# Hybrid attention encoder layer: where row scaling, the eviction of output tiles and the last weight group's sum stand in the order of group B

## The chip, the cores and the metric

The kernel runs on one core of a Trainium2 chip. A core has five engines with a queue each, which meet only through semaphores: TensorE (PE: matrix products into PSUM; its weight loads are listed apart as PEld), VectorE (DVE), ScalarE (ACT), GpSimd (POOL) and SyncE (SP, which here only starts transfers). Sixteen DMA engines move data. The metric is the device time of one launch in microseconds; the median of the runs shown is 554.95 us. "Before" is the kernel without the change, "after" the one with it.

## What is computed

One mixer layer over 1024 tokens of width 1024, token t at row t // 64 and column t % 64 of a grid:

```python
h = _rmsnorm(x, norm_gain[l])
proj = h @ w_in[l]
q_a, k_a, v_a, g_a, q_b, k_b, v_b, g_b = jnp.split(proj, split_at, axis=-1)
...
o_a = _gqa_blocked(q_a, k_a, v_a) * jax.nn.silu(g_a)
o_b = _neighbourhood_attn(q_b, k_b, v_b, na_rpb[l])
o_b = o_b * jax.nn.silu(g_b)
mixed = jnp.concatenate([o_a, o_b], axis=-1)
x = x + mixed @ w_out[l]
...
return _rmsnorm(x, final_norm_gain)
```

Group A is ordinary attention with 8 query heads over all tokens (after a norm and a rotation of q and k). Group B has 8 heads, and each query sees a window of 8 grid rows by 16 columns, with a learned bias. Both are gated, joined, multiplied by `w_out`, added to x and normed.

## The kernel before

**Tiling.** The tokens are cut into 8 blocks u of 128 (8 grid columns each), so that a block of group B needs the keys of at most three blocks. All matrix products run in float16, each operand split into a high and a low part, so that one product takes three matmuls (hi*hi, hi*lo, lo*hi). The weights come in 17 groups of 256 columns: 0 to 12 from `w_in` (0 k/v of A, 1-2 q of A, 3-4 q of B, 5-6 k of B, 7-8 v of B, 9-10 gate of A, 11-12 gate of B) and 13 to 16 from `w_out`.

**A weight group's way.** `load_w(g)` fetches 1 MB and plans `squares` (L366): four quarters, each an ACT `Square` with its row sum (L372). After the fourth, a job puts g on the list `pend`, `delay` slots later (L374). The next `b_scores` (L825), directly behind its own matmuls, takes g from `pend` and runs `prep_b` (L382): four matmuls with one column (L388) add the squares over the partitions, DVE (L390) and POOL (L391) turn that into a scale. Then `split(g)` (L408) plans four `hi` on ACT (L414), each of which plans a `lo` on DVE (L419). When the last `lo` is done, the group is ready, and one slot later group g+2 is fetched. A matmul that needs the group waits for its pieces.

**Group B.** 32 units (u, p), u in the order 0, 7, 1, 2, 3, 4, 5, 6 and p a pair of heads, run in 36 slots. Slot i does, in the order in which instructions are issued:

- what is planned "pre"; then ACT jobs of up to 1.2 us ("early")
- `b_lo` of unit i-1: DVE L863 makes the low part of the probabilities, SP starts their transposing transfer (L878)
- `b_qk` of unit i: TensorE scores (L833, L836), perhaps `prep_b`, DVE bias and minimum (L854, twice), ACT exponentials (L856, twice) and the high part (L858)
- more ACT jobs, then DVE jobs, then what is planned "post"
- a fill of 24 or 30 projection matmuls (L504): first the eight gate tiles of B, then the output rows
- `b_pv` of unit i-3, from slot 18 on i-4: probabilities times values (L896 to L898)

On every engine this program order is kept through slot 35. The trace shows slot i by its L833. TensorE may run ahead of the others: it stops only where it needs something that they have not done. The scores have four PSUM banks (two are used in each slot), the projections two (`pjb`), the values two (`pvb`).

**The planner.** `Flow.job(engine, cost, fn, delay, late)` makes a job due `delay` slots later. `work` (L91) gives ACT 2.85 and DVE 2.45 units a slot (L130: 1.7 + 0.654 * 4.2 less 1.6 or 2.0). What is left from the slot before is carried, but at most half a budget (1.42 for ACT). Jobs are taken by `late` (smallest first), then by due slot, then by number. A job with `late=0` always runs once it is due; another only if half its cost is below what is left. In the early part `work` stops when 1.2 are spent:

```python
self.left[eng] = 1e9 if b is None else min(self.left.get(eng, 0.0), 0.5 * b) + b
stop = -1e9 if early is None else self.left[eng] - early
```

A square L372 of groups 13 to 16 costs 1.0 (`late=1.2`), a `hi` 0.6 (`late=0.5`), a `put` 0.8, the square L933 0.82, each L946 0.72.

**The places that the change touches.**

- `g_gen` (L700), for B: ACT tanh of the gate (L706), then the job `mul` on DVE (L712), which writes the gated values into `mixB` and marks the half row (pair of blocks, 256 columns) ready. L706 and L712 read the projection tile, so L712 sets it free.
- `evac` in `b_pv_head` (L900): for the four heads of a block, DVE takes the reciprocal of the row sums (L905), scales (L906, L908) and POOL multiplies the result into `mixB` (L910). It sets the `pvb` bank free. If the gate isn't ready, the job is planned again for the next slot, at its cost of 0.85, and there it stands before the gate's `mul`, as its number is smaller.
- `os_start` (L920): as soon as both halves of a block are there, the block's joined row is squared (ACT L933, DVE L938, L940), scaled (POOL L941), split (ACT L946, DVE L950) and transposed for the output product (SP L959).
- `out_gen` (L999): output columns of one or two blocks, 48 matmuls into a projection tile. Then, for the first six blocks from slot 18 on, `put` (L1009): ACT takes the tile out (L1013, twice) and POOL adds it to x (L1019). Each puts the next tile's matmuls off until L1013 is done.

## Time and profile before

| | |
|---|---|
| Median of three runs (lowest, highest) | 554.95 us (553.38, 557.83) |
| The profiled execution: its time, its span | 554.79 us, 553.0 us |
| Mean granted clock of TensorE | 0.989 |
| Group A's end and group B's 36 slots | about 363 to 508 us |
| Output product of the last blocks, final norm | 508 to 553 us |
| TensorE busy, 400 to 450 us | 48.51 of 50 us |
| TensorE busy, 450 to 500 us | 45.42 of 50 us |
| TensorE busy, 500 to 553 us | 45.04 of 53 us |
| VectorE busy, 400 to 450 and 450 to 500 us | 45.44 and 42.10 us |
| ScalarE busy, 400 to 450 and 450 to 500 us | 41.60 and 40.21 us |

The span runs from the first to the last instruction; the time of the execution is 1.8 us longer. In the timeline a row is start, duration, engine, line, operation, out<-in, size, count, and in brackets the idle time before it with what ended it. In the view of waits a row is who waited for whom, the total in us, how often, and the longest. In the chain a row is start, duration, engine, tile and line.

### The profile page before, as it was taken

The page shows a single profiled execution, that of the slowest core. Times are in us where ns is not written, and L with a number is a line of the kernel's source. Part 1 is how long each engine was busy: PE and PEld are TensorE (multiplying, and loading weights), DVE is VectorE, ACT ScalarE, POOL GpSimd, SP SyncE. Part 2 cuts the span into 40 slices and gives each one's busy share as a digit, 9 for nine tenths or more (in the row PEclk, how much of TensorE's full clock was granted, in tenths as well). Part 3 has the DMA queues.
Part 4 walks back from the last instruction along what each step waited for, and adds up shares of the span by engine and source line. Part 5 has one row for each costly group of instructions (what it writes and reads, how often), then busy time and mean ns, then how long its engine had stood idle before and what let it go on. Part 6 is the DMA issues. An engine that isn't in the chain of part 4 may idle for free.

```text
span 553.0 us, 12864 instructions
## 1 busy us (share of the span) xinstructions
PE 507.8 (92%) x5071; PEld 397.2 (72%) x5071; DVE 445.3 (81%) x887; ACT 381.4 (69%) x671; POOL 178.9 (32%) x201
## 2 busy tenths in 40 slices
PE   2657889998999999999999999999999998799994
PEld 0446768876887555558888888988777786589883
DVE  4599678889987888879879898867898997887732
ACT  4545465967887868787787696648688788784411
POOL 1385787581110000101000022634433123344510
PEclk9989999999999999999999999999999999999998
DMA  8997837879999999999997999744897799979722
GB/s 243 210 203 216 146 59 181 135 144 176 208 196 217 191 231 186 216 176 178 194 217 143 202 186 200 120 125 71 146 191 138 136 250 202 219 115 204 173 74 76
DMA packets 244509, 95.40 MB, mean 173 GB/s; under 512 B 235489, under 2 KB 236001, under 8 KB 242530
## 3 DMA queue, kind: packets, MB, share of 16 engines
q1 hardware_dynamic: 242434, 81.23, 80.1%
q0 software_dynamic: 1728, 12.58, 7.3%
q8 instruction: 39, 0.64, 0.5%
q10 hardware_dynamic: 288, 0.79, 0.5%
q14 instruction: 20, 0.16, 0.1%
HBM read 29.56 MB, written 4.19 MB: 61 GB/s over the span
## 4 chain that ended last, share of the span: by engine, by line
PE 50%; DVE 10%; ACT 9%; issue 5%; DMA 3%; POOL 0%; DVEq 0%; POOLq 0%; ACTq 0%
PE pj L504 17%; PE kb L504 7%; PE pjb L504 7%; PE pv L775 5%; PE s L741 4%; PE s L743 4%; ACT rq L856 3%; DVE ar L854 3%; ACT ar L858 2%; PE pv L776 2%; PE sb L504 2%; DMA pt<-ar 2%; DVE ar L863 1%; DMA ar<-ar 1%; DVE whl L419 1%
## 5 line engine op out<-in xcount | busy, mean ns | idle before, releaser
L504 PEld LDWEIGHTS <-hT 128*128 128x128 f16 x2112 | 204.2, 99 | 59.5 <-DMA hT<-ar 16.3
L504 PE MATMUL pj<-whl,hT 128*128 128x256 f16 x1680 | 201.7, 278 | 21.8 <-DMA hT<-ar 9.4
L752 ACT ACTIVATE ar<-s,nm,sm 128x1024 f32<-128x1024 f32 x64 | 76.9, 1201 | 47.7 <-DVE nm L748 45.7
L748 DVE CUSTOM_DVE_ANT_0 ar<-s,sm 128x1024 bf16<-128x1024 f32 x64 | 82.0, 1281 | 30.3 <-PE s L743 28.5
L504 PEld LDWEIGHTS <-ar 128*128 128x128 f16 x768 | 73.8, 98 | 16.0 <-issue 7.8
L758 DVE TENSOR_TENSOR ar<-ar 128x1024 f16<-128x1024 f32 x64 | 79.4, 1241 | 1.2 <-ACT ar L753 1.2
L753 ACT ACTIVATE ar<-ar 128x1024 f16<-128x1024 f32 x64 | 67.6, 1057 | 2.3 <-DVE ar L758 0.4
L504 PE MATMUL pjb<-whl,ar 128*128 128x256 f16 x480 | 56.4, 273 | 2.8 <-ACT whl L414 1.5
L856 ACT ACTIVATE rq<-ar,nm 128x384 f32<-128x384 f32 (+1 forms) x64 | 34.0, 579 | 25.7 <-DVE nm L854 25.1
L504 PE MATMUL pjb<-whl,hT 128*128 128x256 f16 x432 | 50.4, 273 | 0.1
L784 POOL TENSOR_TENSOR ar<-ar,sum 128x256 f32<-128x256 f32 x16 | 11.3, 709 | 110.7 <-DVE ar L783 95.3
L504 PE MATMUL kb<-hT,whl 128*128 128x512 f16 x192 | 44.5, 379 | 0.0
L419 DVE SCALAR_TENSOR_TENSOR whl<-raw,sm,whl 128x512 f16<-128x512 f32 x52 | 41.0, 821 | 2.7 <-ACT whl L414 2.7
L775 PE MATMUL pv<-va,ar 128*128 128x128 f16 x384 | 39.1, 220 | 0.0
L863 DVE SCALAR_TENSOR_TENSOR ar<-rq,ar 128x768 f16<-128x768 f32 (+1 forms) x32 | 29.3, 915 | 11.0 <-ACT ar L858 10.6
L741 PE MATMUL s<-kTa,rq 128*128 128x512 f16 x128 | 38.1, 379 | 0.0
L776 PE MATMUL pv<-va,ar 128*128 128x64 f16 x384 | 37.8, 193 | 0.0
L775 PEld LDWEIGHTS <-ar 128*128 128x128 f16 x384 | 33.9, 98 | 5.3
L776 PEld LDWEIGHTS <-ar 128*128 128x128 f16 x384 | 33.2, 98 | 5.3
L414 ACT ACTIVATE whl<-raw,sm 128x512 f16<-128x512 f32 x52 | 34.0, 709 | 1.4 <-POOL sm L391 1.4
L391 POOL TENSOR_TENSOR sm<-wss,mh 128x1 f32<-128x1 f32 x17 | 10.5, 619 | 72.7 <-DVE wss L390 72.7
L910 POOL TENSOR_TENSOR ar<-ar,qkg 128x256 f32<-128x256 f32 x16 | 17.1, 1072 | 51.6 <-DVE qkg L908 36.4
(174 smaller groups left out, 915.9 us busy)
## 6 DMA issues: line engine op xcount, KB each, us to landing
raw<-in_w_dram POOLq DMA_DIRECT2D x11, 1024.0 KB, 7.6
ar<-in_x_dram SPq DMA_DIRECT2D x7, 512.0 KB, 6.1
raw<-in_wo_dram SPq DMA_DIRECT2D x3, 1024.0 KB, 7.0
khh<-ar SPq DMA_DIRECT2D x16, 128.0 KB, 2.7
x2b<-in_x_dram SPq DMA_DIRECT2D x4, 512.0 KB, 7.4
x<-in_x_dram SPq DMA_DIRECT2D x4, 512.0 KB, 5.6
out_dram<-x2b SPq DMA_DIRECT2D x8, 256.0 KB, 4.1
out_dram<-x SPq DMA_DIRECT2D x7, 256.0 KB, 2.9
```

The lines of the kernel that those rows point to most:

```text
L414: act.activation(wp[g][0][:, q], raw[g][:, q], AF.Copy, scale=col(S_ + g))
L419: dve.scalar_tensor_tensor(wp[g][1][:, q], raw[g][:, q], col(S_ + g), wp[g][0][:, q], op0=OP.mult, op1=OP.subtract)
L504: pe.matmul(*o[0], **o[1])
L741: pe.matmul(s[:, c * 512:(c + 1) * 512], q, kTa[:, 4 * c:4 * c + 4, hh], start=True, stop=False)
L748: dve.tensor_tensor_reduce(out=hl[:, 1].bitcast(BF16), in0=s, in1=col(SHA).to_broadcast([P, 1024]), scale=col(NSA), scalar=3e38, op0=OP.ad ...
L752: act.activation(p32, s, AF.Exp, bias=nm, scale=col(SCA), accum_out=rsum[hh, u][:, h:h + 1])
L753: at(0, "mid", lambda: act.activation(hl[:, 0], p32, AF.Copy))
L758: dve.tensor_tensor(hl[:, 1], p32, hl[:, 0], op=OP.subtract)
L775: pe.matmul(o, pt[:, kt], va[:, kt, hh], start=kt == 0, stop=False)
L776: pe.matmul(o[:, :D], pt[:, 8 + kt], va[:, kt, hh, :D], start=False, stop=kt == 7)
L856: act.activation(p32[:, e], t[:, e], AF.Exp, bias=nm, scale=-1.0)
L863: dve.scalar_tensor_tensor(hl[:, 1], p32, 2.0 ** 14, hl[:, 0], op0=OP.mult, op1=OP.subtract)
```

## The change

Four places are edited, which make three parts.

1. *Rows scaled directly behind their gate.* An `evac` whose gate isn't ready is no longer planned again; it is kept in `held` under its half row. The gate's `mul` plans what is held there at once, for the same slot.
2. *Output rows evicted first.* `put` is no longer a job. It is planned "pre" of the next slot, so it comes before all jobs of ScalarE there, and takes 0.8 from what was left before the cap.
3. *Last weight group's sum.* For group 16 the way from the last square to `pend` takes one slot and not two.

```diff
             if i == 3:
-                job("act", 0, pend.append, g, delay=2 if "b" in late else 1, late=0, key=("sq", g))
+                job("act", 0, pend.append, g, delay=2 if "b" in late and g < 16 else 1, late=0, key=("sq", g))
...
-    mixA, mixB = {}, {}
+    mixA, mixB, held = {}, {}, {}
...
                     dve.scalar_tensor_tensor(m, th, 1.0, pt, op0=OP.add, op1=OP.mult)
                     ready.add((up, cols.start))
+                    for e in held.pop((up, cols.start), ()):
+                        job("dve", 0.85, e, delay=0, late=0)
                     return
...
                 if (u // 2, hh * GC) not in ready:
-                    job("dve", 0.85, evac, late=0)
+                    held.setdefault((u // 2, hh * GC), []).append(evac)
                     return
...
             o = late["ov"][:, k % 2]
+            fl.left["act"] = fl.left.get("act", 0.0) - 0.8
             for i in range(2):
                 act.activation(o[:, i], pt[:, i], AF.Copy, scale=rw[:, i:i + 1])
...
             if "ov" in late and jobs[0][0] in ORDER[:6]:
-                job("act", 0.4 * len(jobs), put, late=0)
+                at(1, "pre", put)
             else:
```

## The prediction, made before the changed kernel had run

> **What bounds the kernel now.** I read the page first, then the waits of TensorE over group B, the chain, and last the timelines of the engines around each wait.

> ```profile
> span 553.0 us, 12864 instructions
> PE 507.8 (92%) x5071; PEld 397.2 (72%) x5071; DVE 445.3 (81%) x887; ACT 381.4 (69%) x671; POOL 178.9 (32%) x201
> ```

> TensorE is busy for 92% of the span, so a gain is a TensorE gap that closes. All three edits act from slot 6 of group B on. There the view of waits, asked for TensorE alone from 360 us to the end, has five lines:

> ```profile
> PE pvb L896 <- DVE qkg L908: 2.0, 4, 0.7
> PE pjb L504 <- ACT pt L1013: 1.8, 1, 1.8
> PE pjb L504 <- ACT whl L414: 1.5, 2, 0.7
> PE pjb L504 <- DVE whl L419: 1.3, 2, 0.8
> PE pjb L504 <- DVE ar L712: 0.3, 1, 0.3
> ```

> Together 6.9 us, 1.2% of the span: the bound of what can be won. The first line is the output bank that waits for a row's scaling (`evac`), the second a projection tile that waits for its eviction (`put`), the next two the split of group 16. The change aims at each. The chain says how they hang together:

> ```profile
> 480.09 0.62 ACT whl L414
> 480.73 0.76 DVE whl L419
> 481.54 0.71 PE pjb L504 x5
> ...
> 529.32 6.98 PE pjb L504 x64
> ```

> Up to 481.5 us the chain hops between ScalarE and VectorE; from there to the tail it is TensorE alone. So the time is set by when TensorE leaves the last wait, and then by fixed matmul work. The timeline of TensorE over slots 24 to 29 (slot i starts with L833; 24 is at 457.16, 29 at 482.63):

> ```profile
> 457.57 0.34 PE L836 MATMUL sb<-klo,qTb 64*128 64x384 f16 x2
> 457.84 3.45 PE L504 MATMUL pjb<-whl,ar 128*128 128x256 f16 x30
> 462.37 2.79 PE L504 MATMUL pjb<-whl,ar 128*128 128x256 f16 x24
> 465.54 0.49 PE L833 MATMUL sb<-khh,qTb 128*128 128x384 f16 x2
> 466.23 0.25 PE L388 MATMUL sb<-wss,mh 128*128 128x1 bf16 x4
> 466.35 1.47 PE L504 MATMUL pjb<-whl,ar 128*128 128x256 f16 x12
> 469.62 1.47 PE L504 MATMUL pjb<-rest,ar 128*128 128x256 f16 x12 [1.80 <-ACT pt L1013]
> 471.47 0.49 PE L833 MATMUL sb<-khh,qTb 128*128 128x384 f16 x2
> 476.02 1.48 PE L504 MATMUL pjb<-whl,ar 128*128 128x256 f16 x12
> 482.63 0.49 PE L833 MATMUL sb<-khh,qTb 128*128 128x384 f16 x2
> ```

> And ScalarE and VectorE in the same stretch:

> ```profile
> 457.84 0.82 ACT L1013 ACTIVATE pt<-pjb,rw 128x256 f32<-128x256 f32 x2
> 458.56 0.63 ACT L372 ACTIVATE rest<-raw 128x512 bf16<-128x512 f32 x1
> 461.00 1.12 ACT L856 ACTIVATE rq<-ar,nm 128x384 f32<-128x384 f32 x2 [1.73 <-DVE nm L854]
> 462.90 0.61 ACT L372 ACTIVATE rest<-raw 128x512 bf16<-128x512 f32 x1
> 463.64 0.63 ACT L372 ACTIVATE rest<-raw 128x512 bf16<-128x512 f32 x1
> 464.40 0.63 ACT L372 ACTIVATE rest<-raw 128x512 bf16<-128x512 f32 x1
> 464.93 0.19 ACT L372 ACTIVATION_READ_ACCUMULATOR rest<-raw 128x1 f32 x1
> 468.75 0.82 ACT L1013 ACTIVATE pt<-pjb,rw 128x256 f32<-128x256 f32 x2
> 463.90 0.61 DVE L854 CUSTOM_DVE_ANT_0 ar<-sb,ar,sm 128x384 f32<-128x384 f32 x1
> 478.28 0.99 DVE L419 SCALAR_TENSOR_TENSOR whl<-raw,sm,whl 128x512 f16<-128x512 f32 x1
> ```

> What to see: TensorE has run ahead. Its scores of slot 24 end at 457.8, VectorE reads them at 463.90. ScalarE is still in slot 22's end when TensorE is in slot 24. L388 (TensorE's sum for group 16) sits in slot 26 at 466.23, 1.1 us after the last of the four squares L372 that it reads (465.12), so today it waits for nothing.

> **Part 1: rows scaled behind their gate.** Nothing is added or removed; L905, L906, L908 on VectorE and POOL's L910 move one slot up for the four row halves whose gate is late (slots 7, 9, 11, 13 to 6, 8, 10, 12). The four waits of 2.0 us go. VectorE does the same work a slot sooner. On POOL, L910 now stands before slot 6's and slot 8's two L804 (`narrow`); their sums are wanted two slots later, and a slot lasts about 4 us, so I take nothing. The first two rows' `os_start` comes a slot sooner, and with it two L933, four L946, L938, L950 and the transposes L959. That shuffles ScalarE's order: in slots 10 and 14 the two L946 fill the early 1.2 us and the gate's tanh L706 falls behind the exponentials. The trace shows this order in slot 15 already:

> ```profile
> 423.57 1.32 ACT L946 ACTIVATE mhl<-ar,os 128x512 f16<-128x512 f32 x2
> 426.68 0.67 ACT L706 ACTIVATE ar<-pjb,sm 128x512 f32<-128x512 f32 x1
> 427.38 0.69 DVE L712 SCALAR_TENSOR_TENSOR ar<-ar,pjb 128x512 f32<-128x512 f32 x1 [0.93 <-ACT ar L706]
> 420.77 0.68 DVE L712 SCALAR_TENSOR_TENSOR ar<-ar,pjb 128x512 f32<-128x512 f32 x1
> 433.31 1.32 ACT L946 ACTIVATE mhl<-ar,os 128x512 f16<-128x512 f32 x2
> 434.54 1.11 ACT L856 ACTIVATE rq<-ar,nm 128x384 f32<-128x384 f32 x2
> ```

> So slot 14's L712 slides from 420.77 by about 3 us, TensorE waits for its bank in slot 15, and slot 15 loses its own stall of the same kind. By slot 16 VectorE stands where it stood. Weight group 13 is split one slot sooner (slot 7 takes two L419, as the row's failed attempt no longer eats budget), so SP loads group 15 in slot 9, its squares L372 leave slots 14 and 16, and slot 17's L946 at 433.31 no longer stand behind one. The exponentials at 434.54 waited for these L946: they may start 0.4 us sooner, and that carries. The 2.0 us are worth nothing by themselves, since TensorE only runs further ahead; the 0.4 us of the ScalarE/VectorE loop count. Bounds: 2.0 us gained if the loop follows TensorE, 2.4 us lost if slot 14's delay stays; I take 0.4 gained, by the last rows.

> **Part 2: `put` first in ScalarE's slot.** Same instructions (two L1013, 0.82 us, and POOL's adds; no DMA, the rows of x were loaded before). The put of slot 25 moves from 468.75 to ahead of the square L933 of its slot. But its 0.8 us are now taken from what is left before the cap of half a budget, and the cap gives them back; nor do they count for the early 1.2 us. In slot 23 I get 1.42 + 2.85 = 4.27 after the cap, so two squares go early (3.27, 2.27), and two more fit behind the exponentials (1.27; half a square's cost, 0.5, is below it; 0.27). In the kernel before it was 4.27 - 0.8 - 1.0 early, 1.0 and 1.0 later down to 0.47, too little, and the fourth square went to slot 24. So the fourth square comes one slot sooner. The second early one lies in the 1.73 us idle ahead of 461.00: free.

> **Part 3: the sum.** With the fourth square in slot 23 and a delay of 1, L388 stands in slot 24, not one but two slots sooner, directly behind the scores that TensorE ends at 457.84. TensorE takes its matmuls in order, so it stands until the fourth square is done: 462.90 + 2 x 0.74 = 464.38, less 0.4 from part 1, plus 0.2 for the last L388 and its signal: the fill of slot 24 starts at 464.15 and not at 457.84. That is a new wait of 6.3 us (5 us, should TensorE lose its lead in slot 15). Queued behind it: everything of TensorE; VectorE's L390 and behind that L854 of slot 24, which moves from 463.90 to about 464.6, while the exponentials behind it started at 465.64 anyway.

> What it buys: the split of group 16 is done around 473 for its first two quarters, before TensorE asks, and the put's tile is free. So from 464.15 on TensorE has only work: 482.63 - 457.84 = 24.79 us, less the put's wait in slot 26 (466.35 + 3.17 = 469.52, but 471.47 was reached: 1.95; 3.17 is slot 25's fill and rows, 465.54 - 462.37), less slot 28's waits (476.02 + 3.17 = 479.19 against 482.63: 3.44), less L388's 0.12: 19.28. Slot 29 starts at 464.15 + 19.28 = 483.43, against 482.63.

> **Sum:** 0.8 us later: 6.3 lost, 5.4 got back, 0.1 of L388 moved. The end follows, as TensorE has no wait after it. The profiled execution took 554.79 us (span 553.0 and 1.8 around it), 0.16 below the median of three, 554.95. Forecast 554.8 + 0.8 = 555.6 us. A measurement of this kernel tells about 1%, 5.5 us, from no change: this is no change.

> **Rivals.**

> *The clock falls in the new stall.* The trace has one stall as long:

> ```profile
> 32.62 4.04 PE L504 MATMUL pj<-whl,hT 128*128 128x256 f16 x20 [5.49 <-ACT whl L397]
> 33.00:34.00 1.00, 0.97 (x5) 0.56 (x4) 1.00 (x2) 1.00 (x2) 1.00 (x2) 0.50 1.28 287
> ```

> After 5.49 us idle the granted clock (the column before the last two) was 0.50, and 20 matmuls took 4.04 us, where 24 took 2.79 at 462.37: 20 would be 2.3, so 1.7 us more. Here: 555.6 + 1.7 = 557.3. Against it: a stall of 5 us, broken by the first three sums, may be too short. [...]

> *The sum lands one slot sooner only* (the fourth square stays in slot 24): TensorE stands in slot 25 until 465.4, the put's wait goes, but VectorE's first two pieces of group 16 come where the first comes now, at 478.28, and end near 480 (0.76 each by the chain): with TensorE's last matmuls and rows slot 29 starts at about 480.8, 1.8 us sooner, 553.0. For it: the name of the change. Against it: the budget above.

> *Faster: no stall.* If the squares end before TensorE comes, which needs the loop of ScalarE and VectorE 5 us earlier or TensorE without its lead, all 5.4 us after slot 24 go, and with the 2.0 of part 1 up to 7: 547.5 to 549.4. Against it: 463.90 against 457.57, a lag that part 1 shortens by 0.4.

> *Slower: the stall isn't repaid.* ScalarE now does group 16's L414 in slot 25, ahead of slot 26's L946 and exponentials, and VectorE three L419 there. If this sets the loop back as far as TensorE was, the later waits stay and 6.3 us are lost: 561.1. It decides where slot 28's L854 comes later than TensorE's bank asks. Against it: the three L419 (2.3 us at 0.76) go from slot 27, so the loop has them back by slot 28.

> **How the numbers follow.** Forecast 0.37, the clock 0.25, one slot 0.15, no stall 0.11, not repaid 0.12. Faster by over 1%: 0.11; within: 0.37 + 0.25 + 0.15 = 0.77; slower: 0.12. The likeliest's own range is 554 to 557. The outer two hold 0.23, so the range takes part of each, as stalls repaid by half: 550.5 to 559.5.

> **What would show it.** Right: no wait at L896 for L908 in slots 7 to 13; a wait of TensorE for L712 in slot 15; four L372 in slot 23; L388's last group in slot 24 some 8 us or less behind L833 at 457, with 5 to 6 us of idle; no wait for L1013, L414 or L419 afterwards; slot 29 at about 483. Wrong: the fourth L372 behind slot 23, or L388 without idle, or waits for L419 that stay.

## The result: 0.9% slower

| | before | after |
|---|---|---|
| Median of the 10 runs of the comparison (lowest, highest) | 555.03 us (553.38, 558.01) | 560.34 us (558.02, 564.78) |
| Ratio, 95% interval | | 1.0089 [1.0064, 1.0114] |
| The profiled execution: its time, its span | 554.79, 553.0 us | 562.42, 560.6 us |
| Mean granted clock of TensorE | 0.989 | 0.974 |

The forecast was 555.6 us and no change; the median lies 0.8 us above the range, and the interval leaves 1 out. (The ratio isn't worked out from the two medians alone, which divide to 1.0096.) The profiled execution is 2.1 us above the median of its kernel; the sums below are made from it.

Lines of the changed kernel lie 2 or 3 further down from L833 on: scores L835 and L838, bias L856, exponentials L858, low part L865, the put L1016. The page of after:

```profile
span 560.6 us, 12863 instructions
PE 512.9 (91%) x5071; PEld 400.3 (71%) x5071; DVE 444.4 (79%) x887; ACT 383.1 (68%) x671; POOL 179.9 (32%) x201
```

The view of TensorE's waits from 360 us on (who waited for whom, total us, how often, the longest):

```profile
PE sb L388 <- ACT rest L372: 6.0, 4, 2.4
PE pjb L504 <- DVE ar L712: 5.3, 2, 2.7
```

The waits for a row's scaling, for the put and for group 16's pieces, 6.6 us together, no longer occur; 11.3 us of waits at L388 and for L712 stand in their place. TensorE is also 5.1 us longer busy with the same 5071 matmuls (512.9 against 507.8). The timeline of TensorE shows where, first around the new waits for L712 (slots 11 and 15; slot 16 starts at 430.02):

```profile
406.88 2.12 PE L504 MATMUL pjb<-whl,hT 128*128 128x256 f16 x18 [2.59 <-DVE ar L712]
425.18 4.45 PE L504 MATMUL pjb<-whl,hT 128*128 128x256 f16 x24 [2.68 <-DVE ar L712]
430.70 0.25 PE L388 MATMUL sb<-wss,mh 128*128 128x1 bf16 x4
```

Then over slots 24 to 29:

```profile
461.16 0.48 PE L835 MATMUL sb<-khh,qTb 128*128 128x384 f16 x2
464.36 0.16 PE L388 MATMUL sb<-wss,mh 128*128 128x1 bf16 x1 [2.44 <-ACT rest L372]
465.11 0.16 PE L388 MATMUL sb<-wss,mh 128*128 128x1 bf16 x1 [0.59 <-ACT rest L372]
467.61 0.16 PE L388 MATMUL sb<-wss,mh 128*128 128x1 bf16 x1 [2.33 <-ACT rest L372]
468.37 0.16 PE L388 MATMUL sb<-wss,mh 128*128 128x1 bf16 x1 [0.59 <-ACT rest L372]
468.39 6.03 PE L504 MATMUL pjb<-whl,ar 128*128 128x256 f16 x30
474.80 0.49 PE L835 MATMUL sb<-khh,qTb 128*128 128x384 f16 x2
490.26 0.49 PE L835 MATMUL sb<-khh,qTb 128*128 128x384 f16 x2
```

The fill of slot 24 takes 6.03 us where it took 3.45. The table by stretches (the third column from the right is the granted clock) says why, and the same for the slow fill of slot 15:

```profile
426.00:427.00 1.00, 1.00 (x6) 0.70 (x5) 1.00 (x5) 0.43 (x1) 0.00 (x0) 0.50 0.07 16
428.00:429.00 1.00, 1.00 (x7) 0.69 (x6) 0.79 (x2) 1.00 (x2) 0.63 (x1) 0.50 0.96 188
...
467.00:468.00 1.00, 0.16 (x1) 0.11 (x1) 0.94 (x1) 0.97 (x3) 0.00 (x0) 0.50 1.20 259
472.00:473.00 1.00, 1.00 (x6) 0.73 (x5) 0.61 (x1) 0.57 (x2) 0.00 (x0) 0.50 0.87 287
473.00:474.00 1.00, 1.00 (x8) 0.75 (x6) 0.00 (x0) 1.00 (x4) 0.65 (x1) 0.64 1.25 206
474.00:475.00 1.00, 1.00 (x24) 0.87 (x22) 0.00 (x0) 0.49 (x1) 0.61 (x1) 1.00 1.08 180
```

After a wait of 2.68 us the clock was 0.50 from 426 to past 429, some 3.4 us; in slot 24 it fell while the four waits were still going on and was 0.50 from just before 467 to past 473, some 6.8 us. VectorE shows what this does to its loop with ScalarE. First before's row for slot 16:

```profile
428.86 0.61 DVE L854 CUSTOM_DVE_ANT_0 ar<-sb,ar,sm 128x384 f32<-128x384 f32 x1
```

and then after's rows, in slots 14 (L712), 16, 21, 24 and 25:

```profile
424.44 0.69 DVE L712 SCALAR_TENSOR_TENSOR ar<-ar,pjb 128x512 f32<-128x512 f32 x1 [1.59 <-ACT ar L706]
...
431.02 0.16 DVE L390 TENSOR_SCALAR wss<-sb 128x1 f32<-128x1 f32 x1 [1.43 <-PE sb L388]
431.10 0.61 DVE L856 CUSTOM_DVE_ANT_0 ar<-sb,ar,sm 128x384 f32<-128x384 f32 x1
...
452.80 1.49 DVE L865 SCALAR_TENSOR_TENSOR ar<-rq,ar 128x768 f16<-128x768 f32 x1
455.15 0.62 DVE L856 CUSTOM_DVE_ANT_0 ar<-sb,ar,sm 128x384 f32<-128x384 f32 x1 [0.86 <-DMA ar<-ar]
...
468.64 0.61 DVE L856 CUSTOM_DVE_ANT_0 ar<-sb,ar,sm 128x384 f32<-128x384 f32 x1
475.59 0.62 DVE L856 CUSTOM_DVE_ANT_0 ar<-sb,ar,sm 128x384 f32<-128x384 f32 x1 [2.98 <-PE sb L838]
```

Part 1 brings group 15's sum from slot 18 to slot 16. There TensorE is late with it, VectorE's L390 waits for it 1.43 us, and behind L390 the scores of the slot are read at 431.10 instead of 428.86: the loop is 2.2 us late, where the forecast had it 0.4 us early. In slot 21 it loses 1.5 us more: L865 takes 1.49 us instead of 0.95, as it also does without part 1 (in put_sum, below), and VectorE waits 0.86 us for a transposing transfer (L880). By slot 24 the loop is 4.7 us late (468.64 against 463.90), where the forecast had 464.6. ScalarE's squares of slot 23 come as late:

```profile
462.88 0.82 ACT L1016 ACTIVATE pt<-pjb,rw 128x256 f32<-128x256 f32 x2
463.59 0.62 ACT L372 ACTIVATE rest<-raw 128x512 bf16<-128x512 f32 x1
464.34 0.63 ACT L372 ACTIVATE rest<-raw 128x512 bf16<-128x512 f32 x1
466.85 0.61 ACT L372 ACTIVATE rest<-raw 128x512 bf16<-128x512 f32 x1
467.59 0.63 ACT L372 ACTIVATE rest<-raw 128x512 bf16<-128x512 f32 x1
```

From 468.37 to the tail the chain is TensorE alone. **The balance:** slot 29 starts at 490.26 instead of 482.63, 7.6 us later, and the span is 7.6 us longer. The forecast had 0.8. The fill of slot 24 starts at 468.39 instead of the forecast 464.15: 4.2 us. From there to slot 29 it takes 490.26 - 468.39 = 21.87 us instead of 19.28: 2.6 us. 0.8 + 4.2 + 2.6 = 7.6.

### The profile page after: what moved, and what is told of

It reads as the page before. It is cut to its first block, busy times and chain, and to the rows that moved or that the text cites. A ratio compares the mean times of both kernels' runs of the same rounds, so it can differ in the third digit from the quotient of the medians.

```text
span 560.6 us, 12863 instructions
## 1 busy us (share of the span) xinstructions
PE 512.9 (91%) x5071; PEld 400.3 (71%) x5071; DVE 444.4 (79%) x887; ACT 383.1 (68%) x671; POOL 179.9 (32%) x201
## 5 line engine op out<-in xcount | busy, mean ns | idle before, releaser
L504 PEld LDWEIGHTS <-hT 128*128 128x128 f16 x2112 | 205.0, 100 | 63.9 <-issue 21.4
L504 PE MATMUL pj<-whl,hT 128*128 128x256 f16 x1680 | 202.0, 278 | 20.5 <-DMA hT<-ar 7.6
L504 PEld LDWEIGHTS <-ar 128*128 128x128 f16 x768 | 75.1, 100 | 12.3 <-issue 2.7
L504 PE MATMUL pjb<-whl,ar 128*128 128x256 f16 x480 | 58.3, 280 | 0.0
L504 PE MATMUL pjb<-whl,hT 128*128 128x256 f16 x432 | 52.0, 278 | 5.3 <-DVE ar L712 5.3
L858 ACT ACTIVATE rq<-ar,nm 128x384 f32<-128x384 f32 (+1 forms) x64 | 34.2, 580 | 29.1 <-DVE nm L856 28.4
L504 PE MATMUL kb<-hT,whl 128*128 128x512 f16 x192 | 44.5, 379 | 0.0
L865 DVE SCALAR_TENSOR_TENSOR ar<-rq,ar 128x768 f16<-128x768 f32 (+1 forms) x32 | 32.2, 1006 | 12.8 <-ACT ar L860 12.7
L419 DVE SCALAR_TENSOR_TENSOR whl<-raw,sm,whl 128x512 f16<-128x512 f32 x52 | 40.0, 797 | 1.9 <-ACT whl L414 1.9
L777 PEld LDWEIGHTS <-ar 128*128 128x128 f16 x384 | 34.2, 99 | 5.5 <-issue 0.3
L778 PEld LDWEIGHTS <-ar 128*128 128x128 f16 x384 | 33.5, 98 | 5.5 <-issue 0.3
L414 ACT ACTIVATE whl<-raw,sm 128x512 f16<-128x512 f32 x52 | 34.0, 708 | 1.4 <-POOL sm L391 1.4
L391 POOL TENSOR_TENSOR sm<-wss,mh 128x1 f32<-128x1 f32 x17 | 10.6, 621 | 72.0 <-DVE wss L390 72.0
```

What stands on the lines that cost most here:

```text
L414: act.activation(wp[g][0][:, q], raw[g][:, q], AF.Copy, scale=col(S_ + g))
L419: dve.scalar_tensor_tensor(wp[g][1][:, q], raw[g][:, q], col(S_ + g), wp[g][0][:, q], op0=OP.mult, op1=OP.subtract)
L504: pe.matmul(*o[0], **o[1])
L777: pe.matmul(o, pt[:, kt], va[:, kt, hh], start=kt == 0, stop=False)
L778: pe.matmul(o[:, :D], pt[:, 8 + kt], va[:, kt, hh, :D], start=False, stop=kt == 7)
L858: act.activation(p32[:, e], t[:, e], AF.Exp, bias=nm, scale=-1.0)
```

## The experiments

None of them leaves out or changes a part of the computation. Every ratio is to the kernel before on the same chip. These were on one chip each: rows_only, put_only, sum_only and rows_put; put_sum, put_sum_warm, sum_late and tanh_rows_put; tanh_first, warm, rows_sum and put_fill; after_again, warm_again, after_fill and sum_fill. A span and a wait are always those of the one profiled execution of a kernel, a ratio is that of many runs.

**The parts alone and in pairs.** rows_only has only the edits on `held`, put_only only those on `put`:

```diff
+                    for e in held.pop((up, cols.start), ()):
+                        job("dve", 0.85, e, delay=0, late=0)
```
```diff
-                job("act", 0.4 * len(jobs), put, late=0)
+                at(1, "pre", put)
```

and sum_only only this:

```diff
-                job("act", 0, pend.append, g, delay=2 if "b" in late else 1, late=0, key=("sq", g))
+                job("act", 0, pend.append, g, delay=2 if "b" in late and g < 16 else 1, late=0, key=("sq", g))
```

rows_put, put_sum and rows_sum have two of the three.

> Part 1 alone. Theory (two new stalls of TensorE, one in slot 15 from part 1 and one in slot 24 from parts 2 and 3 together, each with a fall of the clock): the wait for L712 in slot 15 of some 2.7 us stays, the clock falls to 0.5 behind it for about 3 us, slot 16's L854 comes some 2 us late; L388 for group 16 stays in slot 26 and waits for nothing; about 2 us slower than before (557). Rival (part 1 carries all of the loss through the late ScalarE/VectorE loop, the sum is repaid as forecast): about 5 us slower (560).

> Part 2 alone. Theory: the fourth square goes to slot 23, L388 to slot 25, where TensorE waits about 2 us for it, too short for a fall of the clock; the waits for L1013 and for most of L414 and L419 go; about 1 us faster than before (554). Rival (part 1 carries the loss): also within 1 us of before. A third reading, that the eviction ahead of the exponentials holds up the loop, would make it 2 us or more slower.

> Part 3 alone. Theory: the fourth square stays in slot 24, so L388 lands in slot 25, one slot sooner, and TensorE waits there about 3 us; the wait for L1013 goes and that for group 16 shrinks: 1 us faster (554) if the clock holds, 1 us slower (556) if it falls. Rival: no slower than before, whatever the clock does.

> Parts 1 and 2, without 3. Theory: slot 15's stall as in the changed kernel, L388 in slot 25 with a wait of 2 to 3 us; about 2 us slower than before (557), so 3 us better than the changed kernel. Rival: as slow as the changed kernel, 560.

> Parts 2 and 3, without 1. Theory, now that each part alone and parts 1 and 2 together turned out within 0.5% of before: parts 2 and 3 only together bring L388 for group 16 to slot 24, where TensorE waits some 6.5 us, and the clock falls behind that. Stall 6.5, clock 2.6, less the 5.4 of later waits: 3 to 4 us slower than before (559). Rival (it needs part 1 as well, by the late loop): no slower than put_only, 554.

> Parts 1 and 3, without part 2. Theory (parts 2 and 3 only together bring the sum into slot 24): the fourth square stays in slot 24, L388 of group 16 stands in slot 25 and waits 1 to 3 us, no wait for L414 and L419; part 1's waits for L712 in slots 11 and 15 as before: some 1.5 us above part 3 alone, so about 555.5, a ratio of 0.999. Rival (the cost of all three is part 1 with part 3, whatever part 2 does): the ratio is 1.005 or more.

| parts | ratio, 95% | span, us | L388 of group 16: slot, wait | wait for L712 |
|---|---|---|---|---|
| 1 (rows_only) | 1.0036 [1.0005, 1.0067] | 556.9 | 26, none | 3.9 us |
| 2 (put_only) | 0.9966 [0.9927, 1.0004] | 553.5 | 25, 2.0 us | 0.3 |
| 3 (sum_only) | 0.9951 [0.9921, 0.9981] | 552.3 | 25, 1.9 | 0.3 |
| 1, 2 (rows_put) | 0.9959 [0.9933, 0.9985] | 552.2 | 25, 0.9 | 3.7 |
| 1, 3 (rows_sum) | 1.0013 [0.9990, 1.0037] | 553.1 | 25, 0.9 | 3.9 |
| 2, 3 (put_sum) | 1.0028 [0.9992, 1.0065] | 557.1 | 24, 6.6 | 0.3 |
| 1, 2, 3 (after) | 1.0089 [1.0064, 1.0114] | 560.6 | 24, 6.0 | 5.3 |

No part alone moves the time by more than half a per cent. Parts 2 and 3 each bring group 16's sum into slot 25, where it waits up to 2 us; only together do they bring it into slot 24. From rows_put to after, where only group 16's sum, and with it the split behind it, comes a slot sooner, it is 1.3% (1.0089 - 0.9959 = 0.0130; the two intervals combined, ± 0.0036). TensorE's timeline of put_sum shows that the wait and the slow fill need no part 1:

```profile
464.33 0.16 PE L388 MATMUL sb<-wss,mh 128*128 128x1 bf16 x1 [3.38 <-ACT rest L372]
465.09 0.16 PE L388 MATMUL sb<-wss,mh 128*128 128x1 bf16 x1 [0.59 <-ACT rest L372]
465.11 5.70 PE L504 MATMUL pjb<-whl,ar 128*128 128x256 f16 x30
```

Part 1 brings the waits for L712 with it wherever it stands, here in the timeline of rows_only for slot 11, where 18 matmuls took 3.54 us instead of 2.12:

```profile
408.62 3.54 PE L504 MATMUL pjb<-whl,hT 128*128 128x256 f16 x18 [2.59 <-DVE ar L712]
```

**The sum two slots later.** The whole change, with group 16's delay at 3, so that L388 stands in slot 26 as before:

```diff
-                job("act", 0, pend.append, g, delay=2 if "b" in late and g < 16 else 1, late=0, key=("sq", g))
+                job("act", 0, pend.append, g, delay=(2 if g < 16 else 3) if "b" in late else 1, late=0, key=("sq", g))
```

> The changed kernel with the delay for group 16 at 3 in place of 1, so that L388 stands in slot 26 as before. Theory: no wait at L388; the waits for L414 and L419 in slot 28 return (3 us); part 1's stalls stay: 556 to 557, 4 us better than the changed kernel. Rival (parts 1 and 2 carry the loss): as slow as the changed kernel.

1.0000 [0.9956, 1.0044]. L388 waits for nothing, and waits for L419 (1.6 us) and L414 (0.6) are back; behind them the next two L835 take 0.83 us, where the two of the slot before took 0.49. The loss of the whole change is gone with the sum's place in slot 24, and so is most of what the early split had bought.

**The tanh first.** The gate's tanh L706 of group B is taken ahead of the L946 in ScalarE's early part; without the sum (tanh_rows_put) and with the whole change (tanh_first):

```diff
-            job("act", 0.7, tanh, late=0)
+            job("act", 0.7, tanh, late=-1 if isb else 0)
```

> Parts 1 and 2 (delay 2, L388 in slot 25), and the gate's tanh ahead of the splits L946 in ScalarE's early part. Theory: the waits for L712 in slots 11 and 15 go, with them the fall of the clock; but TensorE comes earlier to L388 in slot 25 and waits there some 2 us more, as the loop of ScalarE and VectorE isn't faster: 1 to 2 us better than rows_put (554). If TensorE is what binds: 3 us or more better.

> All three parts, and the gate's tanh L706 of group B ahead of the L946 in ScalarE's early part. Theory (part 1's cost inside the whole is the wait for L712 in slots 11 and 15, which drops the clock and sets the loop of ScalarE and VectorE back): no wait of TensorE for L712 above 1 us, the clock stays at 1.0 in slots 11 to 16, the loop stands in slot 24 as it does with parts 2 and 3 alone; the 6 us stall at L388 in slot 24 and its 2 us at half clock stay. So about 557.5, a ratio of 1.003. Rival (the loop falls behind for other reasons that part 1 brings, so that the waits for L712 are a sign and not the cause): the waits go and the time stays at 560, 1.009.

tanh_rows_put: 0.9975 [0.9940, 1.0009], not to be told from rows_put; its waits for L712 shrink to 2.3 us, and the wait at L388 in slot 25 grows from 0.9 to 1.7. The fall of the clock isn't gone: it no longer comes in slot 11 (18 matmuls in 2.13 us), but behind these 1.7 us, where the clock is 0.70 in the mean from 465 to 470 us and 24 matmuls take 4.45 us instead of 2.79:

```profile
464.01 4.45 PE L504 MATMUL pjb<-whl,ar 128*128 128x256 f16 x24
```

tanh_first: 1.0060 [1.0036, 1.0084]. Its waits of TensorE and VectorE's slot 16:

```profile
PE sb L388 <- ACT rest L372: 6.8, 4, 3.3
PE pjb L504 <- DVE ar L712: 2.3, 3, 1.0
```
```profile
428.93 0.61 DVE L856 CUSTOM_DVE_ANT_0 ar<-sb,ar,sm 128x384 f32<-128x384 f32 x1
```

The scores of slot 16 are read at 428.93, as before (428.86), and not at 431.10; the clock is 1.00 from 400 to 440. So the 2.2 us there go with the long wait for L712 in slot 15 and the half clock behind it; after_again, below, which has neither, lacks them too. The span is 2.9 us shorter than after's. In the ratio it is 0.003 less than all three parts, half of what was expected, and the intervals of the two overlap. Of the 4.7 us in slot 24 about 2.2 stay (466.15 against 463.90). put_sum, without part 1, has 1.5 of them (465.36), and most of the rest is VectorE's wait for a transposing transfer in slot 21, here 0.69 us, which before and put_sum don't have. It comes in some profiles with part 1 and not in others; why, no run took apart.

**The clock kept up.** 176 matmuls of 64 columns, whose result nothing reads, run in slot 24 ahead of group 16's L388; with parts 2 and 3 (put_sum_warm) and with the whole change (warm, and again as warm_again beside the whole change, after_again, on one chip):

```diff
             g = pend.pop(0)
+            if g == 16:
+                for _ in range(176):
+                    pe.matmul(at_s[:, 432:496], q[hs[0]], khh[:, hs[0], :64], start=True, stop=True)
```

> Parts 2 and 3, with 176 small matmuls (64 columns, into an unused piece of a score bank, read by nobody) directly ahead of L388 in slot 24. They add nothing where TensorE stands anyway. If the clock is a cost of its own, it stays at 1.0 in slot 24 and the fill there takes 3.3 us instead of 5.9: 2.6 us faster than put_sum. If the stall alone counts: the same time as put_sum.

> All three parts, and 176 matmuls of 64 columns into an unread part of the scores bank ahead of group 16's L388 in slot 24. Theory (the stall's price is its length plus about 2.3 us at half clock behind it): clock 1.0 from 462 to 475, slot 24's fill of 30 matmuls in 3.45 us and not 6.03, the end 2.3 us sooner than with all three parts: 558, a ratio of 1.005. Rival (the half clock is hidden, as TensorE would wait later for what it now reaches late): the fill in 3.45 us, but a wait for L414, L419 or L1016 returns behind it and the ratio stays at 1.009.

> All three parts, unchanged, on the same chip as the next three. Both theories: a ratio of 1.009, within 1.006 to 1.012; the profile with a wait of 2.6 us for L712 in slots 11 and 15, the clock at half behind one of them, and a stall of 6 us at L388 in slot 24 with the clock at half behind it.

> The kernel with 176 dummy matmuls in slot 24's stall once more, beside all three parts on the same chip. Theory (half a clock for 6.5 us costs what the matmuls in it take longer): 2.3 to 2.6 us below all three parts, 0.004 to 0.005 in the ratio, so 1.004 to 1.005. Rival (in most runs the half clock is paid elsewhere or hidden): within 0.002 of all three parts, 1.007 to 1.009.

| | ratio, 95% | with the dummies |
|---|---|---|
| put_sum, put_sum_warm | 1.0028 [0.9992, 1.0065] | 1.0000 [0.9967, 1.0034] |
| after, warm | 1.0089 [1.0064, 1.0114] | 1.0080 [1.0056, 1.0104] |
| after_again, warm_again | 1.0100 [1.0072, 1.0129] | 1.0066 [1.0043, 1.0090] |

The end of the fourth square, the sums and slot 24's fill in warm's timeline:

```profile
467.03 0.19 ACT L372 ACTIVATION_READ_ACCUMULATOR rest<-raw 128x1 f32 x1
468.15 0.24 PE L388 MATMUL sb<-wss,mh 128*128 128x1 bf16 x4
468.25 3.44 PE L504 MATMUL pjb<-whl,ar 128*128 128x256 f16 x30
```

The fill starts about as late as in after (468.39), takes 3.44 us again, and the clock is 1.00 from 460 to 480. The spans are 558.0 and 556.3 us against 560.6 and 558.5: 2.6 and 2.2 us less (556.0 against 557.1 for parts 2 and 3, where slot 24 began 1.1 us later with the dummies). The three differences of the ratios, 0.0028, 0.0009 and 0.0034, are weaker; weighted by their intervals they make 0.0022 ± 0.0023, 1.2 us. The profiles show the price of the half clock; the ratios neither confirm 2.3 us nor rule it out. They also hold a cost of the dummies: in warm the fourth square was done at 467.22 and in warm_again at 465.19, but L388 came behind the dummies at 468.15 and 466.51, 0.9 and 1.3 us later. That the half clock is not in the profiled executions alone, the mean clock listed for every run shows: taken as either full or half, 2 x (1 - clock) x span estimates 28.5 us at half clock in the mean of after_again's runs and 18.8 in warm_again's, 25.0 in put_sum's and 19.1 in put_sum_warm's.

after_again's profile shows how two executions of one kernel come to differ by 2 us in span: there the clock fell behind the wait in slot 11 (2.56 us; 0.66 in the mean from 405 to 410 us, 18 matmuls in 3.57), which made slot 12 later and the wait in slot 15 shorter (1.22 us), and the clock stayed up behind that one (1.00 from 425 to 430 us); slot 16 started at 427.86 instead of 430.02. VectorE's slots 16 and 21:

```profile
429.09 0.61 DVE L856 CUSTOM_DVE_ANT_0 ar<-sb,ar,sm 128x384 f32<-128x384 f32 x1
453.68 0.62 DVE L856 CUSTOM_DVE_ANT_0 ar<-sb,ar,sm 128x384 f32<-128x384 f32 x1 [1.36 <-DMA ar<-ar]
```

The scores of slot 16 are read on time (before: 428.86), yet by slot 21 the loop is 2.5 us late (before: 451.20), more than half of it the wait for the transfer. Slot 24's fill starts at 466.90 and slot 29 at 488.10, so the balance is 0.8 + 2.75 + 1.92 here. With 560.30 us this execution is nearer to its kernel's median (560.71) than after's; the 2.2 us of slot 16 belong to after's profile and not to every execution.

**The sum behind a fill.** Here the slot's projection matmuls run between the scores and group 16's L388; with the whole change in slot 24 (after_fill), with part 3 alone in slot 25 (sum_fill):

```diff
+        self.n = n
         self.run("pre")
...
-        self.fill(n)
+        self.fill(self.n)
...
             g = pend.pop(0)
+            if g == 16:
+                fl.fill(fl.n)
+                fl.n = 0
```

> All three parts, but TensorE does slot 24's fill (30 matmuls, 3.45 us) ahead of group 16's L388 and not behind them; the squares and the split stay in their places. Theory (the loss is TensorE's stall): the stall is 3.4 us shorter, 2.5 to 3 us, what follows the fourth square is shorter by the fill, and with a stall that short the clock may stay up: 3.4 to 6 us below all three parts, a ratio of 0.998 to 1.003. Rival (the loop of ScalarE and VectorE behind slot 24 sets the end): TensorE waits for L414, L419 or L1016 later, and the ratio stays within 0.002 of all three parts.

> Part 3 alone, but TensorE does slot 25's fill (24 matmuls, 2.79 us) ahead of group 16's L388. Theory: the wait of 1.9 us at L388 goes, no wait for L414 or L419 comes; up to 1.9 us below part 3 alone, so about 552.5 to 554, a ratio of 0.992 to 0.995, below 1 with its interval. Rival (TensorE comes sooner to the same wait for the put L1013 in slot 28, which grows from 1.8 to 3.7): the time of part 3 alone, 0.995 to 0.998.

after_fill: 1.0007 [0.9985, 1.0029], where after_again on the same chip has 1.0100 [1.0072, 1.0129]: 0.9% or 5.2 us won back by one fill of 3.45 us put ahead of four tiny matmuls. In these kernels some lines have moved: L389 is the sum's L388, L373 the square L372, L505 the fill's L504, L1017 in sum_fill the put, L860 in put_fill the bias. after_fill still waits 3.7 us for the gate's L712; its other wait, and TensorE's slots 24 and 25:

```profile
PE sb L389 <- ACT rest L373: 2.9, 2, 2.3
```
```profile
461.91 3.60 PE L505 MATMUL pjb<-whl,ar 128*128 128x256 f16 x30
468.66 0.16 PE L389 MATMUL sb<-wss,mh 128*128 128x1 bf16 x1 [0.59 <-ACT rest L373]
469.98 4.36 PE L505 MATMUL pjb<-whl,ar 128*128 128x256 f16 x24
```

Slot 24 begins at 461.23, as in after (461.16), slot 29 at 486.32 instead of 490.26. No wait for L414, L419 or the put comes back, so the loop of ScalarE and VectorE isn't the bound there: the price is TensorE's wait, with the clock behind it. Behind this wait of 2.9 us the clock still falls in this profile, the slowest of its 12 runs (0.68 in the mean from 470 to 475 us, 24 matmuls in 4.36 us instead of 2.79).

sum_fill: 0.9997 [0.9973, 1.0020]; the mechanism of its rival came true. The wait at L388 is gone, and TensorE comes sooner to the put:

```profile
PE pjb L505 <- ACT pt L1017: 4.0, 2, 2.5
```

4.0 us instead of 1.8 for part 3 alone. By the ratios it is slower than part 3 alone (0.9951, on another chip), which neither theory had, though its profiled span is shorter (550.9 against 552.3 us); that stays open. put_fill moved the sum with part 2 alone to the very end of slot 25, behind the values:

```diff
-            g = pend.pop(0)
-            prep_b(g, at_s[:, 400 + g:401 + g])
-            try_split(g)
+            if pend[0] == 16:
+                at(0, "end", last_sum, at_s)
+            else:
+                last_sum(at_s)
```

> Part 2 alone, and group 16's four L388 with its L390 and L391 issued at the end of slot 25, behind its fill and its values, and not behind its scores. Theory (where the sum stands in TensorE's order sets its price): L388 waits for nothing, the 2.0 us wait of part 2 alone goes, ScalarE's four L414 stay in slot 26, so nothing later moves: up to 2 us below part 2 alone, 552.5 to 554, a ratio of 0.994 to 0.997. Rival (TensorE only runs further ahead and waits the same 2 us at L896, L1014 or L419 behind it): the same time as part 2 alone, 0.997, with longer waits there.

0.9994 [0.9974, 1.0014]. L388 writes into a scores bank; issued behind VectorE's reads of that bank (L860) it waited 4.4 us for them here, though it touches other columns:

```profile
PE sb L388 <- DVE nm L860: 4.4, 1, 4.4
```

A longer wait in place of the one of 2.0 us, and half a clock behind it (12 matmuls in 2.46 us instead of 1.48); neither theory had it. The row names the reads that ended the wait; what put the dependency there, no run shows. No kernel here is shown to beat before by more than half a per cent; the best, part 3 alone with 0.9951, was compared once, and sum_fill, which waits less at L388, shows no gain.

## Why the prediction was wrong, by its steps

- **Part 2 and the budget: right.** Two squares stand ahead of slot 23's exponentials and two behind, the put first, and L388 is in slot 24 as forecast.
- **Part 3, the stall and what it buys: right.** TensorE was idle 6.0 us at L388 (forecast 6.3). In after that is partly luck: TensorE came to slot 24 4.0 us later than in before (461.16 against 457.16), and the squares were late by as much. put_sum, where TensorE is on time (457.24), confirms it without luck: 6.6 us. The later waits for the put, L414 and L419 went in full: from the stall's end to slot 29 it took 21.87 us, and without the 2.58 that the fill was slower 19.29, where 19.28 was forecast. With that the rival "not repaid" falls. That the sum lands one slot sooner only, another rival, is what each of parts 2 and 3 does alone.
- **Part 1, "TensorE waits for its bank in slot 15, and slot 15 loses its own stall of the same kind. By slot 16 VectorE stands where it stood": wrong, 4.2 us.** This is the step that failed: the wait was given no price, and 0.4 us of gain stood in the sum. L712 of slot 14 came at 424.44, about as forecast (420.77 plus some 3), and TensorE waited 2.68 us for it. But behind that the clock was 0.50 for some 3.4 us, and group 15's sum, whose move to slot 16 the prediction leaves out, came late; VectorE waited 1.43 us for it at L390, ahead of the scores. The loop lost 2.2 us there and more up to slot 21, and the stall in slot 24 ended 4.2 us later than forecast. The wait in slot 11, 2.59 us, was not forecast at all. In after_again, where the clock fell in slot 11, the same term is 2.75 us without the loss in slot 16, and part of the cause, the later transfer in slot 21, stays open. By the ratios part 1 adds 0.0061 to parts 2 and 3 (1.0089 - 1.0028, ± 0.0044), 0.0062 to part 3 and 0.0036 to nothing; added to part 2 alone it adds nothing (0.9966, 0.9959).
- **The clock: left out of the sum, as a rival at 1.7 us and a chance of 0.25; it came, at 2.6 us in the profile.** The first sums in the stall broke its idle time into 2.44, 0.59, 2.33 and 0.59 us, which the prediction thought might be too short; the clock was 0.50 from just before 467 us all the same. The row from 33 us, with half a clock behind 5.49 us, was the right one to go by, but there the half clock lasted 3.4 us, which cost its 20 matmuls the 1.7. In slot 24 it lasted 6.8 us, and 5.3 of them lay behind the stall.
- **"The 2.0 us are worth nothing by themselves": right.** The four waits at L896 went, and no gain came of it.

In the profile the forecast of 0.8 us became 0.8 plus 4.2 plus 2.6. In both places a wait of TensorE was taken for free or for its length alone. The ratios put the miss on part 1: parts 2 and 3 without it cost 0.0028, 1.6 us (± 2.0), where the prediction's sum without part 1's 0.4 is 1.2, and part 1 adds 3.4 us (± 2.5) to them. Two of the prediction's sums are off in the last digit (464.38 - 0.4 + 0.2 is 464.18; 554.8 less 7.4 is 547.4), which changes nothing.

## What to carry to other kernels

A reduction of four tiny matmuls, placed in TensorE's order where its input was not ready, held up everything behind it here for 6.0 us, and one fill of 3.45 us moved ahead of it was worth 0.9%. Each of two edits may bring such a sum nearer at little cost (0.9966 and 0.9951 here), and both together bring it to a place where its input is far from ready (1.0028); so the pair has to be priced, not each alone. And a wait of TensorE is priced with the matmuls behind it, which took up to 6.03 us instead of 3.45 here, and with the engines that need its next small result (VectorE stood 1.43 us at L390), not with its idle time alone.

## What the runs showed of the hardware

In slot 24 of after, after_again, put_sum and tanh_first the half clock lasted some 6.8 us (in after_again 0.90, 0.50 and 0.92 in the means of the three stretches of 5 us from 460 to 475); there it had begun 1.5 to 2.9 us before the stall ended, and behind the waits for L712 at most 0.6 us before their end. Four single-column matmuls in slot 24's stall did not prevent it: in after the clock was 0.50 from just before 467 to past 473 us. With 176 matmuls of 64 columns it did not come, though TensorE stood 1.2 to 1.9 us among them: the clock was 1.00 from 460 to 475 us in put_sum_warm, warm and warm_again.
